# Conv feed-forwards and latent stage on normalized inputs: later splits, projections by token tile, gains in the weights

## The chip, the cores and the metric

The kernel runs on one core of a Trainium2 chip, as one program. The metric is the device time of one execution in microseconds (us); smaller is better. The engines are TensorE (PE in the profile; PEld are its weight loads), VectorE (DVE), ScalarE (ACT), GpSimd (POOL) and SyncE (SP), which starts the transfers of the weights. Each engine takes its own instructions in a fixed order and waits on semaphores for the others.

## What is computed

Two transformer blocks run one after the other on 256 tokens of width 1024, in fp32. The first has two layers of feed-forward, three-branch attention and feed-forward. The second has a convolutional mixer, a convolutional feed-forward, a latent attention and a second convolutional feed-forward. Cut to the parts that the change touches:

```
def conv_ffn(x_n, w_up, conv_w, w_down):            # w_up 1024 x 5632, w_down 2816 x 1024
    g, u = split(causal_dwconv(x_n @ w_up, conv_w)) # three taps along the tokens
    return (silu(g) * u) @ w_down

h = h + short_conv_mixer(rms_norm(h, a_mix_norm), ...)
h = h + conv_ffn(rms_norm(h, ffn_norm[0]), ...)
ckv = rms_norm(h, kv_in_norm) @ w_dkv               # 256 latent columns and 64 rope columns
k_nope, v = rms_norm(ckv[:256], kv_norm) @ w_ukv;   k_rope = rope(ckv[256:])
q = rms_norm(rms_norm(h, b_mix_norm) @ w_dq, q_norm) @ w_uq   # 8 heads, 128 + 64 rope
s = (q_nope . k_nope + q_rope . k_rope) * scale     # causal, one k_rope for all heads
h = h + (softmax(s) @ v) @ w_o
h = h + conv_ffn(rms_norm(h, ffn_norm[1]), ...)
return rms_norm(h, final_norm)
```

In the mixers of the first block one of the branches is stick-breaking attention: log-sigmoids of the scores are summed from the right along the keys, and the weights are the exponentials of those sums.

## The kernel before

**Products.** Every large product is made as three matmuls of numbers that are split into a high and a low part: `hi` x `acth`, `lo` x `acth` and `hi` x `actl`. The weights come in pieces of 512 KB. For each, SP starts the transfer to `raw`, ScalarE casts it to `hi` (line 270), VectorE subtracts (`lo`, line 271). There are five buffers for `raw` and eight each for `hi` and `lo`. Activations are split in the same way (lines 375 and 376, on ScalarE and on VectorE or POOL). The 256 tokens are two tiles of 128, t = 0 and t = 1. In the form of `mm_b` a product has the weights stationary and streams 256 token columns; in the form of `mm_a` the activations are stationary and 512 weight columns are streamed into the banks named `acc00`, `acc01` (t = 0) and `acc10`, `acc11` (t = 1). PSUM has four banks for products (tag mm), two for scores (z) and two for transposes (tr).

**Order.** TensorE's order is set by the Python code itself: a simulated clock `now` advances with each matmul group (`tick`), and side work stands in generators (`Task`) that give up control with a delay from the table `DELAY`. When the clock reaches a task's due time, its next part is emitted there. The other engines' orders come from the tile scheduler.

**Stick-breaking** (`stick_breaking`): scores of a key block and a query block for eight heads go into two z banks (line 592); ScalarE and VectorE make the log terms (lines 608 to 612, 585, `lnh` and `lnl` in 375 and 376); the last of them frees the bank. `sums` are matmuls with a triangle (line 624). In between stand the projections of the mixer, evicted as qs, ks, qf, kf (line 816). `sb_z`, `sb_ln` and so on are the delays between these steps.

**Conv feed-forward** (`conv_ffn`): the input is multiplied by the gain but not by the row factor r of the norm. Chunks c = 0 to 3 are made in `mm_a` form and transposed; chunks 4 to 21 in `mm_b` form, each into one bank `cf` (gate half and up half, 48 matmuls). VectorE multiplies it by r into `cgu` (line 972), where r lies along the columns in `rb`, which `across` makes with two diagonal matmuls (line 484). ScalarE multiplies by the last tap (line 877), VectorE adds the other two (line 879, 255 and 254 columns, for gate and up), ScalarE takes silu (line 945), POOL multiplies gate and up (line 946), and the product is split. Behind chunk 21 the down projection begins (`out_proj`): its four accumulators take the banks of chunks 18 to 21.

**Latent** (`latent`): `both` transposes h and makes two inputs, with the gains of the two norms. The first projections (`dkv`, 320 columns; `dq`, 512) run over both token tiles each, the row factor is applied behind them (`factor`), then come the norms, rope, transposes, `uk`, `uqr`, `uqn` and `uv`. `latent_half` and `latent_unit` make the scores: for each head a matmul of 128 rows (kn, line 1085) and one of 64 rows (kr, line 1086) into one z bank. `pre_gain` and `pre_norm` prepare the next stage's input at the end of `out_proj`; the delays `n_conv`, `n_ffnA`, `n_mla`, `n_ffn2` say how much later the transposes are asked for.

## Time and profile before

| quantity | value |
|---|---|
| median of three timed runs | 1906.56 us (1905.06 to 1908.55) |
| profiled execution | 1908.66 us |
| its span | 1906.9 us |
| mean granted TensorE clock | 0.991 of full speed |
| PE busy | 1868.0 us (98%) |
| DVE busy | 1260.4 us (66%) |
| ACT busy | 969.1 us (51%) |
| POOL busy | 256.7 us (13%) |

Busy time of TensorE is modelled from overlapping matmuls, so 98% does not say how much of it is useful: a matmul of 512 columns stands with about 0.4 us, while two of them begin 0.23 us apart. What TensorE loses is seen in the distance of starts, in its waits, and in stretches where the granted clock is below 1.

### The profile page before, as it was taken

The numbers are of one execution on the slowest core, as the hardware profiler recorded it, in microseconds if no ns is written. First come the engines' busy times: TensorE is split into PE (matmuls) and PEld (weight loads), VectorE is DVE, ScalarE is ACT, GpSimd is POOL, SyncE is SP. The second block draws the span as 40 slices with busy tenths as digits, with TensorE's granted clock in tenths as the row PEclk, the third lists the DMA queues.
The fourth block names the chain that finished last, engine by engine and source line by source line (L and its number), as shares of the span: only waits on it lengthen the run. The fifth ranks groups of instructions, "written<-read, shape, count | busy, mean of one in ns | idle before, by whom it ended". The sixth has DMA issues, their size and how long they took to land.

```text
span 1906.9 us, 30378 instructions
## 1 busy us (share of the span) xinstructions
PE 1868.0 (98%) x11990; PEld 1674.8 (88%) x11990; DVE 1260.4 (66%) x1682; ACT 969.1 (51%) x1483; POOL 256.7 (13%) x231
## 2 busy tenths in 40 slices
PE   8999999999999999999999999999999989999988
PEld 7998998878899889989887889988989977889976
DVE  6664756766766476637776776647668756658763
ACT  6444545554644364436555464435456544547552
POOL 1000102002100010001200210001414313003320
PEclk9999999999999999999999999999999999999989
DMA  8655664335555565546443555545454444425551
GB/s 288 220 195 181 227 209 162 143 133 200 206 186 184 177 213 185 188 166 248 163 143 133 210 192 192 184 169 202 177 192 174 178 178 152 152 92 189 178 178 65
DMA packets 95358, 343.30 MB, mean 180 GB/s; under 512 B 10720, under 2 KB 10992, under 8 KB 95216
## 3 DMA queue, kind: packets, MB, share of 16 engines
q1 hardware_dynamic: 95216, 341.37, 51.3%
q8 instruction: 94, 1.54, 0.3%
q14 instruction: 48, 0.39, 0.1%
HBM read 339.21 MB, written 2.11 MB: 179 GB/s over the span
## 4 chain that ended last, share of the span: by engine, by line
PE 84%; DVE 7%; ACT 3%; POOL 3%; issue 2%; DMA 0%; DVEq 0%; SPq 0%; ACTq 0%; POOLq 0%
PE acc L287 14%; PE acc L290 14%; PE acc L288 14%; PE gu L299 7%; PE gu L300 7%; PE gu L298 7%; DVE lo L271 3%; PE mm L298 3%; PE mm L299 3%; PE mm L300 3%; DVE cy L879 2%; ACT hi L270 2%; POOL cy L946 2%; PE tr L383 2%; PE cv L300 1%
## 5 line engine op out<-in xcount | busy, mean ns | idle before, releaser
L271 DVE TENSOR_TENSOR lo<-raw,hi 128x1024 fp32r<-128x1024 f32 (+3 forms) x616 | 759.3, 1241 | 342.4 <-ACT hi L270 340.8
L270 ACT CAST hi<-raw 128x1024 fp32r<-128x1024 f32 (+3 forms) x616 | 639.5, 1043 | 451.1 <-PE acc L290 218.5
L287 PE MATMUL acc<-hi,acth 128*128 128x512 f32 x1200 | 483.8, 403 | 12.6 <-DVE cgu L972 11.0
L288 PE MATMUL acc<-lo,acth 128*128 128x512 f32 x1200 | 476.3, 397 | 0.2 <-DVE lo L271 0.2
L290 PE MATMUL acc<-hi,actl 128*128 128x512 f32 x1200 | 388.2, 397 | 0.6 <-DVE actl L376 0.5
L300 PE MATMUL gu<-acth,lo 128*128 128x256 f32 x1152 | 323.8, 281 | 0.0
L299 PE MATMUL gu<-actl,hi 128*128 128x256 f32 x1152 | 323.6, 281 | 0.0
L298 PE MATMUL gu<-acth,hi 128*128 128x256 f32 x1152 | 323.3, 281 | 0.0
L287 PEld LDWEIGHTS acc<-hi,acth 128*128 128x128 f32 x1200 | 227.5, 190 | 67.8 <-DVE cgu L972 12.3
L290 PEld LDWEIGHTS acc<-hi,actl 128*128 128x128 f32 x1200 | 227.0, 189 | 55.6 <-DVE actl L376 2.3
L288 PEld LDWEIGHTS acc<-lo,acth 128*128 128x128 f32 x1200 | 227.3, 189 | 50.5 <-DVE lo L271 0.9
L298 PEld LDWEIGHTS gu<-acth,hi 128*128 128x128 f32 x1152 | 216.9, 188 | 0.2
L299 PEld LDWEIGHTS gu<-actl,hi 128*128 128x128 f32 x1152 | 216.8, 188 | 0.2
L300 PEld LDWEIGHTS gu<-acth,lo 128*128 128x128 f32 x1152 | 216.8, 188 | 0.0
L400 POOL TENSOR_TENSOR r<-v,mhalf 128x1 f32<-128x1 f32 x40 | 51.3, 1281 | 931.4 <-DVE v L397 923.1
L298 PE MATMUL cf<-acth,hi 128*128 128x256 f32 x576 | 162.1, 282 | 0.0
L300 PE MATMUL cf<-acth,lo 128*128 128x256 f32 x576 | 161.9, 281 | 0.0
L299 PE MATMUL cf<-actl,hi 128*128 128x256 f32 x576 | 161.8, 281 | 0.0
L298 PE MATMUL mm<-acth,hi 128*128 128x256 f32 x432 | 124.0, 287 | 0.0
L300 PE MATMUL mm<-acth,lo 128*128 128x256 f32 x432 | 122.6, 284 | 0.0
L299 PE MATMUL mm<-actl,hi 128*128 128x256 f32 x432 | 122.5, 284 | 0.0
L298 PEld LDWEIGHTS cf<-acth,hi 128*128 128x128 f32 x576 | 108.5, 188 | 0.1
(235 smaller groups left out, 2302.5 us busy)
## 6 DMA issues: line engine op xcount, KB each, us to landing
raw<-ffn_gu SPq DMA_DIRECT2D x175, 512.0 KB, 3.8
raw<-ffn_dn SPq DMA_DIRECT2D x88, 512.0 KB, 3.3
raw<-cf_up SPq DMA_DIRECT2D x88, 512.0 KB, 3.5
raw<-gate SPq DMA_DIRECT2D x48, 512.0 KB, 3.2
raw<-cf_dn SPq DMA_DIRECT2D x44, 512.0 KB, 3.4
raw<-a_in SPq DMA_DIRECT2D x18, 512.0 KB, 4.6
gain<-gains SPq DMA_DIRECT2D x17, 512.0 KB, 5.1
raw<-in_v SPq DMA_DIRECT2D x16, 516.0 KB, 3.3
```

The source lines that it names most:

```text
L270: self.last_hi = nc.scalar.copy(out=hi[:, cs], in_=raw[:, cs])
L271: nc.vector.tensor_tensor(out=lo[:, cs], in0=raw[:, cs], in1=hi[:, cs].bitcast(F32), op=ALU.subtract)
L287: nc.tensor.matmul(ps, x.h(k, ts), hi[:, cs], start=first, stop=False)
L288: nc.tensor.matmul(ps, x.h(k, ts), lo[:, cs], start=False, stop=False)
L290: nc.tensor.matmul(ps, x.l(k, ts), hi[:, cs], start=False, stop=last)
L298: nc.tensor.matmul(ps, hi[:, c], x.h(k), start=k == 0, stop=False)
L299: nc.tensor.matmul(ps, hi[:, c], x.l(k), start=False, stop=False)
L300: nc.tensor.matmul(ps, lo[:, c], x.h(k), start=False, stop=k == nk - 1)
L383: self.nc.tensor.transpose(ps[:, w * P:w * P + P], n[:, c * P:c * P + P], self.ident)
L400: nc.gpsimd.tensor_tensor(out=r, in0=v, in1=self.mhalf, op=ALU.pow)
L879: nc.vector.scalar_tensor_tensor(out=y[:, i:], in0=ps[:, :S - i], scalar=w[2 - i], in1=y[:, i:], op0=ALU.mult, op1=ALU.add)
L946: nc.gpsimd.tensor_tensor(out=y[:, 0], in0=y[:, 0], in1=y[:, 1], op=ALU.mult)
```

## The change

The change has five parts.

- **Delays.** In the table, `sb_z` goes from 9000 to 13000 and `sb_ln` from 9000 to 6000; `merge`, `n_conv`, `n_ffnA`, `n_mla`, `kv`, `q` and `lat_gap` change, `n_ffn2` is set apart for each layer (8300 and 6500), and `cf_gated` and `cf_split` are new. In the mixer's merge one of two additions moves from POOL to VectorE.
- **Conv feed-forward.** The input is normalized in full (`pre_norm`), so `r`, `across` and the product into `cgu` go. The convolution reads the PSUM bank itself. Its last-tap products stand first for gate and up, then both other taps of gate, then both of up. The product of gate and up and its split are tasks of their own. The down projection takes the first four chunks of t = 0 before t = 1 (`head=4`).
- **Latent input.** `plain` makes one normalized input; the gains of the two norms go into the weights (`take_gained`). `dkv` and `dq` run on t = 0, then on t = 1.
- **Latent rope.** The rope part of the keys is doubled before rope; `uqr` runs for each token tile by itself.
- **Latent scores.** They are made for two heads at a time, u = 0 and u = 1, in two z banks; the two 64-row matmuls, on the upper and the lower rows, stand next to each other. `latent_out` sets the order of the output projection.

```diff
-    DELAY = dict(..., merge=4600, ..., sb_z=9000, sb_ln=9000, ...
-                 cf_gap=4100, kv=6700, q=2600, rope=5600, lat_gap=2200, lat_p=9000, n_conv=4000, n_ffnA=1500,
-                 n_mla=3000, ..., n_ffn2=8300)
+    DELAY = dict(..., merge=3000, ..., sb_z=13000, sb_ln=6000, ...
+                 cf_gap=4100, cf_gated=2000, cf_split=9500, kv=5500, q=4000, rope=5600, lat_gap=6000, lat_p=9000, n_conv=9000,
+                 n_ffnA=5500, n_mla=7500, ..., n_ffn20=8300, n_ffn21=6500)
...
+    def take_gained(self, src, i, gains, w):
...
+        for j, g in enumerate(gains):
+            cs = slice(j * w, j * w + w)
+            nc.scalar.mul(out=hi[:, cs], in_=raw[:, cs], mul=g)
+            nc.vector.scalar_tensor_tensor(out=lo[:, cs], in0=raw[:, cs], scalar=g, in1=hi[:, cs].bitcast(F32),
+                                           op0=ALU.mult, op1=ALU.subtract)
...
-                        nc.gpsimd.tensor_tensor(out=gates[0][t][:, cs], in0=gates[0][t][:, cs], in1=y, op=ALU.add)
+                        (nc.gpsimd if i == 1 else nc.vector).tensor_tensor(out=gates[0][t][:, cs], in0=gates[0][t][:, cs], in1=y, op=ALU.add)
...
         def finish(c, gu):
             y = self.t2(name="cy", shape=(2, S))
-            for i in range(2):
-                self.conv3(y[:, i], gu[:, i], PP_FCONV + 132 * l + 3 * (c + KF * i))
+            for part in (self.conv3_last, self.conv3_rest):
+                for i in range(2):
+                    part(y[:, i], gu[:, i], PP_FCONV + 132 * l + 3 * (c + KF * i))
             nc.scalar.activation(out=y[:, 0], in_=y[:, 0], func=AF.Silu)
+            made[c] = [self.spawn(gated(c, y), self.DELAY["cf_gated"])]
+
+        def gated(c, y):
             nc.gpsimd.tensor_tensor(out=y[:, 0], in0=y[:, 0], in1=y[:, 1], op=ALU.mult)
+            yield self.DELAY["cf_split"]
             self.split([d[:, 0] for d in hT.blocks(c, 1)], y[:, 0], nc.gpsimd)
...
-            gu = self.t2(name="cgu", shape=(2, S))
-            nc.vector.tensor_tensor(out=gu, in0=bank, in1=rb, op=ALU.mult)
-            finish(c, gu)
-        return self.out_proj(dsrc, KF, hT, None, nxt)
+            finish(c, bank)
+        return self.out_proj(dsrc, KF, hT, None, nxt, before=made, head=4)
...
+        for t in range(NT):
+            self.join(ready[t])
+            for i, (src, per, w, g0, then, tasks) in enumerate(((s_dkv, 3, 320, PP_KV, kv, tkv), (s_dq, 2, 512, PP_Q, qlat, tq))):
+                chunks = kept[i] if t else [lambda i=i, c=c: keep(i, c) for c in self.whole(src, KD, per, gains=g0)]
+                tasks.append(self.spawn(then(t, rows(x, chunks, t, w))))
...
-            nc.tensor.matmul(z[:, i], qn[e][:, j, t * P:t * P + P], kn[e][:, j, :n], start=True, stop=False)
-            nc.tensor.matmul(z[:, i], qr[rows, j, t * P:t * P + P], kr[rows, :n], start=False, stop=True)
+                for u in range(2):
+                    nc.tensor.matmul(zs[u][:, i], qn[e][:, 2 * i + u, ts], kn[e][:, 2 * i + u, :n], start=True, stop=False)
+                for u in range(2):
+                    rows = slice(64 * u, 64 * u + 64)
+                    nc.tensor.matmul(zs[u][:, i], qr[rows, 2 * e + i, ts], kr[rows, :n], start=False, stop=True)
...
+        x2, g2 = Act(self, KD), self.gain("ffnA")
+        ready = self.conv_mixer(*state, lambda t: self.pre_norm(t, g2, x2, self.DELAY["n_conv"]))
...
+        def plain(t):
+            r = self.row_rstd(self.h[t])
+            ns = [self.nrm() for _ in range(2)]
+            for a in range(2):
+                nc.scalar.mul(out=ns[a], in_=self.h[t][:, a * 512:a * 512 + 512], mul=r)
             yield self.DELAY["n_ffnA"]
+            for a in range(2):
+                self.transpose_split(ns[a], x3.part(4 * a, 4, t))
```

**The order on TensorE, stick-breaking of the first layer.** The first z matmuls of the scores (0,1) stand on TensorE behind these products; `mm_3161` and `mm_3224` are the banks of two neighbouring blocks of the projections. Before:

```order
L298 MATMUL mm_3161<-acth_146,hi_3187 128x256
L299 MATMUL mm_3161<-actl_148,hi_3187 128x256
L300 MATMUL mm_3161<-acth_146,lo_3188 128x256
L592 MATMUL z_3198<-qs_2781,ks_2925 128x128
L592 MATMUL z_3199<-qs_2781,ks_2925 128x128
```

After:

```order
L313 MATMUL mm_3224<-acth_147,hi_3219 128x256
L314 MATMUL mm_3224<-actl_149,hi_3219 128x256
L315 MATMUL mm_3224<-acth_147,lo_3220 128x256
L609 MATMUL z_3243<-qs_2781,ks_2925 128x128
L609 MATMUL z_3244<-qs_2781,ks_2925 128x128
```

The scores moved from the middle of one block into the next one, 36 matmuls of 256 columns later.

**The order on VectorE at the same place.** `lnl_3083` is the operation that frees the second of the two z banks; lb and z with the number 3081 and 3061 are of the scores ahead, those with 3208 and 3198 (3253 and 3243) of the scores (0,1). Before:

```order
L611 SCALAR_TENSOR_TENSOR lb_3081<-z_3061,lb_3081 128x512
L612 TENSOR_TENSOR z_3061<-lb_3081,z_3061 128x512
L271 TENSOR_TENSOR lo_3495<-raw_3493,hi_3494 128x1024
L585 TENSOR_TENSOR z_3061<-z_3061,cst_88 128x512
L376 TENSOR_TENSOR lnl_3083<-z_3061,lnh_3082 128x512
L611 SCALAR_TENSOR_TENSOR lb_3208<-z_3198,lb_3208 128x512
L816 SCALAR_TENSOR_TENSOR qf_3092<-mm_3161,rb_2563 128x512
```

After:

```order
L628 SCALAR_TENSOR_TENSOR lb_3081<-z_3061,lb_3081 128x512
L629 TENSOR_TENSOR z_3061<-lb_3081,z_3061 128x512
L271 TENSOR_TENSOR lo_3495<-raw_3493,hi_3494 128x1024
L602 TENSOR_TENSOR z_3061<-z_3061,cst_88 128x512
L833 SCALAR_TENSOR_TENSOR qf_3092<-mm_3161,rb_2563 128x512
L271 TENSOR_TENSOR lo_3526<-raw_3524,hi_3525 128x1024
L393 TENSOR_TENSOR lnl_3083<-z_3061,lnh_3082 128x512
```

One eviction (qf) and one `lo` now stand ahead of `lnl_3083`.

**The order on VectorE, one round of the conv feed-forward's stream.** `cy` is a chunk's convolution, gate and up halves in turn. Before:

```order
L879 SCALAR_TENSOR_TENSOR cy_14705<-cgu_14703,pp_89,cy_14705 128x255 x2
L879 SCALAR_TENSOR_TENSOR cy_14705<-cgu_14703,pp_89,cy_14705 128x254 x2
L271 TENSOR_TENSOR lo_15015<-raw_15013,hi_15014 128x1024
L972 TENSOR_TENSOR cgu_14777<-cf_14716,rb_13948 128x512
L271 TENSOR_TENSOR lo_15045<-raw_15043,hi_15044 128x1024
```

After:

```order
L898 SCALAR_TENSOR_TENSOR cy_14814<-cf_14750,pp_89,cy_14814 128x255
L898 SCALAR_TENSOR_TENSOR cy_14814<-cf_14750,pp_89,cy_14814 128x254
L898 SCALAR_TENSOR_TENSOR cy_14814<-cf_14750,pp_89,cy_14814 128x255
L898 SCALAR_TENSOR_TENSOR cy_14814<-cf_14750,pp_89,cy_14814 128x254
L271 TENSOR_TENSOR lo_15113<-raw_15111,hi_15112 128x1024
L271 TENSOR_TENSOR lo_15146<-raw_15144,hi_15145 128x1024
```

The product into `cgu` is gone, the multiply-adds alternate in another way and read the bank, and the two `lo` of a round are neighbours. On ScalarE the order of a round is the same in both kernels: last taps, `hi`, silu, `acth`, `hi`.

## Rows read from the trace of the kernel before

**Rows 1.** Waits of TensorE: line, who ended them, total us, times, longest

```profile
PE acc L287 <- DVE cgu L972: 11.0, 3, 5.2
PE z L592 <- DVE lnl L376: 6.4, 2, 3.2
...
PE tr L383 <- DVE kr L1019: 1.8, 1, 1.8
...
PE tr L383 <- DVE cp L895: 1.0, 1, 1.0
PE tr L383 <- DVE h L459: 0.9, 1, 0.9
...
PE tr L383 <- ACT cb L896: 0.7, 1, 0.7
...
PE ca L287 <- ACT acth L375: 0.5, 1, 0.5
```

**Rows 2.** Stretches: busy us (instructions) of PE, PEld, DVE, ACT, POOL; PEclk; DMA

```profile
300.00:320.00 20.00, 16.80 (x125) 16.28 (x124) 12.54 (x16) 11.08 (x17) 0.00 (x0) 0.83 0.29 103
920.00:940.00 20.00, 16.80 (x133) 16.28 (x132) 13.26 (x17) 10.99 (x17) 0.00 (x0) 0.91 0.31 106
...
1320.00:1340.00 20.00, 18.30 (x136) 17.63 (x135) 13.86 (x21) 9.59 (x15) 5.82 (x5) 0.91 0.66 241
...
1595.00:1620.00 25.00, 21.43 (x107) 17.78 (x106) 21.39 (x38) 12.87 (x24) 13.27 (x20) 0.93 0.58 192
```

**Rows 3.** Timeline of PE, first layer: start, us, instruction, count, idle before

```profile
305.40 0.48 PE L592 MATMUL z<-qs,ks 64*128 64x128 f32 x2
```

**Rows 4.** Timeline of DVE, stick-breaking of the first layer

```profile
305.77 1.23 DVE L271 TENSOR_TENSOR lo<-raw,hi 128x1024 fp32r<-128x1024 f32 x1 [0.22 <-ACT hi L270]
...
308.25 0.69 DVE L376 TENSOR_TENSOR lnl<-z,lnh 128x512 fp32r<-128x512 f32 x1 [0.65 <-ACT lnh L375]
...
345.51 0.69 DVE L376 TENSOR_TENSOR lnl<-z,lnh 128x512 fp32r<-128x512 f32 x1 [0.65 <-ACT lnh L375]
346.46 1.29 DVE L626 TENSOR_TENSOR lb<-tr,lb 128x512 f32<-128x512 f32 x2 [0.25 <-PE tr L624]
```

**Rows 5.** Timeline of PE, conv mixer: the matmuls of one across

```profile
1324.21 0.61 PE L484 MATMUL tr<-diag,ones 128*128 128x128 f32 x4
```

**Rows 6.** Timeline of PE: scores of fox heads, then of latent heads

```profile
357.93 1.16 PE L592 MATMUL z<-kf,qf 64*128 64x128 f32 x16
...
1644.99 0.49 PE L1085 MATMUL z<-kn,qn 128*128 128x128 f32 x2
1645.41 0.48 PE L1086 MATMUL z<-kr,qr 64*128 64x128 f32 x2
```

**Rows 7.** Timeline of PE: last chunk of the first conv feed-forward, down projection

```profile
1526.84 0.28 PE L300 MATMUL cf<-acth,lo 128*128 128x256 f32 x1
...
1528.26 0.28 PE L300 MATMUL cf<-acth,lo 128*128 128x256 f32 x1
...
1535.53 0.80 PE L287 MATMUL acc<-hi,acth 128*128 128x512 f32 x1 [5.14 <-DVE cgu L972]
```

**Rows 8.** Timeline of DVE in the last rounds of that stream

```profile
1532.08 1.66 DVE L879 SCALAR_TENSOR_TENSOR cy<-cgu,pp,cy 128x255 f32<-128x255 f32 x4
1533.66 1.22 DVE L271 TENSOR_TENSOR lo<-raw,hi 128x1024 fp32r<-128x1024 f32 x1
1534.79 0.68 DVE L972 TENSOR_TENSOR cgu<-cf,rb 128x512 f32<-128x512 f32 x1
...
1538.02 1.66 DVE L879 SCALAR_TENSOR_TENSOR cy<-cgu,pp,cy 128x255 f32<-128x255 f32 x4
```

**Rows 9.** Timeline of POOL in the same rounds

```profile
1533.93 1.52 POOL L946 TENSOR_TENSOR cy<-cy 128x256 f32<-128x256 f32 x1 [3.15 <-ACT cy L945]
```

**Rows 10.** Timeline of DVE, conv mixer: two multiply-adds, the second on the first's result

```profile
1335.89 1.00 DVE L879 SCALAR_TENSOR_TENSOR cz<-cp,pp,cz 128x255 f32<-128x255 f32 x2 [1.17 <-ACT cz L877]
```

**Rows 11.** Timeline of POOL behind the first mixer: the power of a norm

```profile
486.97 6.01 POOL L400 TENSOR_TENSOR r<-v,mhalf 128x1 f32<-128x1 f32 x1 [5.18 <-DVE v L397]
```

More of the change, by code (lines that the diff above doesn't have):

```diff
@@ L354, in rows_a, with whole @@
             done(t)
-    def whole(self, src, nk, per=1, parts=1):
+    def whole(self, src, nk, per=1, parts=1, gains=None):
         kept = {}
@@ L361, in one @@
             if k % per == 0:
-                kept[0] = self.take(src, k // per, parts if k == 0 else 1)
+                g = gains and [self.pp[:, gains + j:gains + j + 1] for j in range(k, min(k + per, nk))]
+                kept[0] = self.take(src, k // per, parts if k == 0 else 1) if g is None else self.take_gained(src, k // per, g, src.shape[2] // per)
             w = src.shape[2] // per
@@ L1040, in latent @@
         self.join(*tq)
[L1041 to L1050 removed]
+        tr.append(self.spawn(qrope(1, rows(cq, uqr, 1, 512))))
         qn = [self.t4(name="qn") for _ in range(2)]
@@ L1056, in latent @@
         self.v_done = []
-        att = [self.spawn(self.latent_half(0, qn, kn, qr, kr, v, x))]
+        units, second = [[], []], []
+        scores = self.spawn(self.latent_scores(units, second, qn, kn, qr, kr, v, x))
+        self.cols_b(s_uqn, range(4, 8), cq, 4, 2, put(qn, nc.scalar.copy))
+        second.append(True)
         ps3, outs3 = self.banks(2)
@@ L1078, in latent_unit @@
[L1078 to L1089 removed]
+        return self.latent_out(s_o, x, units, nxt)
@@ new lines, in latent_out, with row, then @@
+    def latent_out(self, src, x, units, nxt):
+        ps, outs = self.banks(2)
+        chunks, held, tasks, done = self.whole(src, KD), [], [], [0, 0]
+        made = lambda e: len(units[e]) == 4 and not any(t.alive for t in units[e])
+        def row(t, os=None, k=None):
+            if k is None:
+                k = done[t]
+                done[t] += 1
+            if k == len(held):
+                held.append(chunks[k]())
+            self.mm_a(os or outs[t], x, k, t, *held[k], first=k == 0, last=k == KD - 1)
+        def then(t):
+            self.residual(t, ps[t], None)
+            yield from nxt(t)
+        self.until(lambda: made(0))
+        for k in range(4):
+            row(0)
+        while done[1] < 4 and not made(1):
+            row(1)
+        self.until(lambda: made(1))
+        for t in range(NT):
+            while done[t] < KD - self.FINE:
+                row(t)
+            for o in outs[t]:
+                for k in range(KD - self.FINE, KD):
+                    row(t, [o], k)
+            tasks.append(self.spawn(then(t)))
+        return tasks
@@ L1092, in latent_unit @@
             yield 400
-        h0 = 4 * e + j0
-        yield from self.weighted("lat", p, sums, nh, n, lambda a, i: v[a][:, h0 + i], P, x.part(h0, nh, t))
+        ts = slice(t * P, n)
+        yield from self.weighted("lat", p, sums, 2, n, lambda a, i: v[a][:, 4 * e + 2 * i + u], P, [y[e][:, u:4:2, ts] for y in (x.hi, x.lo)])
     def run(self, out):
```

155 lines of the change are left out of this document (73 added, 82 removed).

## The prediction

> **What bounds the kernel now.** The profiled execution took 1908.66 us with a span of 1906.9 us; the median of the three timed runs is 1906.56 us, 2.1 us less. I make the sum against 1908.66 and take 2.1 us off at the end. TensorE is the bound nearly everywhere: in the stream of a conv feed-forward two starts of 256-column matmuls lie 0.118 us apart, twelve of them from 1526.84 to 1528.26 [rows 7], and nothing on other engines shows as a wait. So only what shortens TensorE's own work, or the places where it stands, can pay. I read the waits of TensorE first [rows 1]. The reader should see that few places hold most of them: three waits of the down projection (acc) for a DVE operation of the conv feed-forwards, cgu, 11.0 us; two of the stick-breaking scores (z) for lnl, 6.4 us; then the conv mixer's head (cp, cb) and the latent stage's (kr). Second view, the same stretches with the granted clock [rows 2]: after each stop the mean clock of the stretch is below 1, so a wait costs more than its length. For 300 to 320 that is 3.2 us of waiting and up to 0.17 x 20 = 3.4 us of slower clock.
>
> **Stick-breaking, both layers.** The scores of block (0,1) move behind 36 more 256-column matmuls, 36 x 0.118 = 4.2 us. They need two z banks, and the second is freed by the lnl that begins at 308.25 and ends at 308.94 [rows 4]. Without the stop TensorE would come there 4.2 us later than the 305.4 of before [rows 3], at 309.6. If lnl stayed where it is, the whole wait would go. It does not stay: the order of the changed kernel puts one more eviction (qf) and one more lo ahead of it. That lo can run only when TensorE has given a weight buffer back. At TensorE's pace, one piece of weights per 24 matmuls or 2.8 us, it comes 2.8 us after the lo of 305.77 [rows 4], at 308.6, and lnl ends at about 308.6 + 1.2 + 0.7 = 310.5. So 0.9 us of the wait stays. Behind it the sums of (0,0) keep their place while the scores (0,0) come 6 matmuls, 0.7 us, later; there the last lnl ends at 346.20 and its reader's result is there at 346.46 [rows 4], so the margin is about nil and some 0.7 us of new waiting is likely. Per layer I count 2.5 us left. Before, waiting and clock cost 6.6 us in the first layer and 3.2 + 0.09 x 20 = 5.0 in the second: together a gain of 4.1 + 2.5 = 6.6, **take -7**, bounds 0 (the wait moves whole) and -10.
>
> **Conv mixer's head.** The layer-1 FFN's last transposes come earlier on TensorE's order, those of cp and cb 20 matmuls later (some 2.2 us of cover against waits of 1.0 and 0.7). With 0.5 for the transposed normal rows and 0.09 x 20 = 1.8 us of clock [rows 1, 2] that is 4.0; leaving 0.4, **-3.6**, bounds -4 and 0. Merge: one addition goes from POOL to DVE and the transposes come 6 matmuls earlier in each mixer; no row prices that, so I take for each the 0.5 that TensorE waited for acth at the conv mixer [rows 1]: **-1**, bounds -1.5 and 0. Two "across" steps go, each one group of four diag matmul records, 0.61 us [rows 5]: **-1**.
>
> **Latent stage.** The rows hold one normalized input in place of two gained ones, and the first projections run on one token tile and then the other, so the work of tile 0 covers the chain of tile 1. The stretch 1595 to 1620 lost 1.8 us to kr, 0.9 to h, and 0.07 x 25 = 1.8 to the clock [rows 1, 2]: 4.5. Each chain (squares, power, scaling, rope, transposes) is still there and fits its cover by 0 to 2 us, so I leave 0.8: **-3.7**, bounds -4.5 and +1. The scores: a kr matmul has 64 rows. Before, each stands between two full-height ones and takes 0.42 us from start to start, as the kn ones do [rows 6]. In the fox heads pairs on the two row halves run side by side: 16 records, eight pairs, in 1.16 us [rows 6]. The change makes such pairs of kr: 8 x 0.42 become 4 x 0.42 for tile 0, 1.7 us saved, and for tile 1, at twice the columns, between 1.7 and twice that. **Take -4.5**, bounds 0 (they accumulate on another matmul's result, which no pair of before does) and -6.
>
> **Later transposes at two boundaries.** The normal rows of the conv feed-forwards are now transposed at the end of the stage ahead (n_conv, n_mla), and TensorE takes the first acth right behind them, as at the conv mixer's head, where it waited 0.5: **+0.7 each, +1.4**, bounds 0 and +4.
>
> **The conv feed-forwards.** This is the large unknown. TensorE makes a chunk in 48 x 0.118 = 5.68 us. The other engines need 5.94 us: the multiply-adds of one chunk begin at 1532.08, those of the next at 1538.02 [rows 8]. So they fall behind by 0.26 us a chunk, and at the end the down projection, which needs the four banks, stands 5.14 us [rows 7] until cgu of the last chunk has read its bank at 1534.79 to 1535.47 [rows 8]. The round is a ring in order of the engines' own programs: acth, hi, lo, the four multiply-adds, silu, POOL's product, acth. cgu, 0.68 us, is not in it, so its removal shortens nothing there. Two things change. (a) The multiply-adds come in the order gate, gate, up, up: each second one needs the first one's result. A dependent pair takes 1.00 us [rows 10], four independent ones 1.66 [rows 8]; four in the new order make about 1.90, and POOL now follows the last of them instead of silu on the third. The product starts at 1532.08 + 1.90 + 0.06 = 1534.04 where it started at 1533.93; lo stands directly behind the multiply-adds as before (1533.66, 0.08 before their end), so it would run from 1533.90 to 1535.12, and the product ends 0.57 after lo, as it does now (1535.45 against 1534.88 [rows 8, 9]): 1535.69, 0.24 later. The ring grows to **6.18 us**. That splits are asked for later (cf_gated, cf_split) doesn't break it: in the built order of ScalarE, acth still stands directly behind silu. (b) A bank is now free after the last multiply-add and not after cgu: at 1539.68 instead of 1535.47 [rows 8], 4.2 us later, and the ring adds 0.24 x 13 = 3.1 over the 13 last chunks, in which the lag grows steadily. So the last bank comes at 1542.8. Against that stands the new order of the down projection: 18 more matmuls of 512 columns on the first two banks, 18 x 0.236 = 4.3 us, so TensorE, which came at 1535.53 - 5.14 = 1530.4, arrives at 1534.7 and stands 8.1 us instead of 5.14. **+3.0 in each feed-forward, +6**. If the multiply-adds kept 1.66, the release is at 1539.7 and the wait 5.0: no change. If POOL's product were not held up (0.74), the ring would fit into 5.68 and the wait would be gone.
>
> **Sum.** -7 - 3.6 - 1 - 1 - 3.7 - 4.5 + 1.4 + 6 = -13.4, so 1895.3 us on the profiled execution's scale and **1893 us** on that of the median.
>
> **Rivals.** *One: the lag in the conv feed-forwards goes away.* For it: lo A may come behind the product where hi is late, and multiply-adds that read PSUM may leave POOL alone. Against: lo has its operands before the multiply-adds end. It would give back the two long waits, 5.14 and 5.2, and by the clock after the stick-breaking waits some 4 us more, instead of +6: 1893 - 20 = 1873. *Two: the stick-breaking wait moves whole* to its sums or stays: 1900. *Three, slower: POOL's product is held up by two lo in a row.* In the new order lo A and lo B are neighbours on DVE, since cgu no longer parts them, and POOL waits long behind such rows: the power for a norm took 6.01 us at 486.97 [rows 11]. Then the ring is 6.18 + 1.23 = 7.41, another 1.23 x 13 = 16 us per feed-forward, 1893 + 32 = 1925; it decides from a ring of about 6.8 us on (26 x 0.66 = 17). Against it: lo B needs hi B, which on ScalarE stands behind acth, which needs the product. *Four: the power starves.* The new normalization puts it on the way at three boundaries, up to 5.5 us more each: 1893 + 16 = 1909, no change. Against it: behind the power's input on DVE stand the scalings that need its result, with one lo between at most, so there is no row of lo to wait for. The Trainium skill, page "SBUF — State Buffer", section "SBUF: two separate sides", says that the port pair shared by VectorE and GpSimd is an exclusive lock: whichever starts first has it for the whole instruction. By that the power would wait for one lo, 1.2 us, and 1909 would be 1897; the 6.01 us of [rows 11] is longer than any one lo, so the trace does not agree here, and I keep 5.5 as the bound.
>
> **How the numbers follow.** About 0.2%, 3.8 us, is what a measurement of this kernel can tell from no change. Chances: the forecast 0.58 (its own range 1885 to 1901), rival one 0.14, two 0.12, three 0.07, four 0.09. Faster: the first three, less a part of two, 0.83; within 0.2%: four and that part, 0.08; slower: three, and four with other costs at their upper bounds, 0.09. For 8 in 10 the range takes in rival one's partial form and two with the boundaries at their upper bounds, up to just below no change: 1875 to 1906.
>
> **What would show it.** Right: two stick-breaking waits under 1.5 us each; acth to acth 6.1 to 6.3 us in the conv feed-forwards and waits of acc for the last multiply-add of 7 to 10 us; kr matmuls starting in pairs; no waits for cp and cb. Wrong: acc waits under 3 us (rival one), TensorE standing inside the cf stream (three), rows of the power above 3 us followed by a wait of tr (four).

## The result and the profile after

The changed kernel takes 1896.57 us (median of four runs, 1895.62 to 1896.99), the kernel before 1906.89 us beside it. The ratio is 0.9945 with a 95% interval of 0.9928 to 0.9963: 10.3 us or 0.55% faster. The forecast was 1893 us, 13.6 us faster than before. The profiled execution of the changed kernel took 1896.99 us.

The head of the page of the changed kernel:

```profile
span 1895.2 us, 30338 instructions
...
PE 1858.4 (98%) x11982; PEld 1665.5 (88%) x11982; DVE 1235.9 (65%) x1657; ACT 966.7 (51%) x1496; POOL 228.5 (12%) x205
```

The waits of TensorE in the changed kernel, to be held against [rows 1] (line, who ended them, total us, times, longest):

```profile
PE acc L302 <- DVE cy L898: 11.8, 3, 5.5
...
PE z L1147 <- ACT p L576: 2.6, 3, 1.4
PE acc L305 <- DVE actl L393: 1.8, 4, 0.9
PE tr L641 <- DVE lnl L393: 1.7, 4, 0.6
PE acc L302 <- ACT acth L392: 1.6, 3, 0.7
PE tr L595 <- DVE actl L393: 0.9, 1, 0.9
PE z L609 <- DVE lnl L393: 0.9, 2, 0.4
...
PE tr L641 <- ACT lnh L392: 0.6, 2, 0.3
```

The waits for kr, cp, cb and h are gone, z for lnl is down from 6.4 to 0.9. The long wait of the down projections stays (11.8 against 11.0), now for the last multiply-add of a chunk. New are waits of the latent scores for the softmax (p). The stretches in question, as in [rows 2] (busy us of PE, PEld, DVE, ACT, POOL, then PEclk, the granted clock as a share of 2.4 GHz):

```profile
300.00:320.00 20.00, 19.57 (x164) 18.98 (x163) 15.66 (x21) 12.02 (x18) 0.00 (x0) 1.00 0.41 138
920.00:940.00 20.00, 19.56 (x165) 18.97 (x164) 15.18 (x20) 12.24 (x18) 0.00 (x0) 1.00 0.47 158
1300.00:1320.00 20.00, 20.00 (x138) 18.44 (x137) 16.24 (x23) 14.03 (x20) 1.38 (x2) 1.00 0.84 287
1520.00:1540.00 20.00, 14.42 (x54) 10.99 (x53) 11.98 (x15) 9.83 (x15) 4.26 (x5) 0.83 0.46 158
1640.00:1660.00 20.00, 15.84 (x79) 10.70 (x79) 13.14 (x35) 10.39 (x35) 0.00 (x0) 0.91 0.23 79
1680.00:1700.00 20.00, 18.46 (x81) 14.56 (x80) 12.77 (x18) 8.70 (x16) 2.02 (x2) 0.91 0.33 107
```

The clock is full where stick-breaking and the conv mixer's head slowed it before, and below 1 in two new places, 1640 to 1660 and 1680 to 1700. At the down projection (1520 to 1540) it is 0.83 in both kernels.

Where the time went, by stage. For each I took the start of the last addition into h (VectorE, the residual of t = 1) in both traces; the column on the right is what the stage gained (-) or lost (+):

| stage | before ends | after ends | gain of the stage | predicted |
|---|---|---|---|---|
| mixer, layer 0, from 207.84 / 208.54 | 500.01 | 496.50 | -4.2 | -4.6 |
| mixer, layer 1, from 861.51 / 857.90 | 1122.11 | 1114.49 | -4.0 | -3.4 |
| FFN of layer 1 and conv mixer | 1401.18 | 1391.12 | -2.4 | -3.6 |
| conv feed-forward 0 | 1600.36 | 1588.96 | -1.3 | +3.2 |
| latent | 1702.64 | 1688.38 | -2.9 | -8.2 |
| conv feed-forward 1 | 1900.08 | 1888.41 | +2.6 | +3.2 |

The predicted column puts the terms of the sum where they fall: half of each -1 (merge, across) and of +6 and +1.4 on each of the two places. For the start of the second mixer I took the addition of t = 0 (861.51 and 857.90). By the starts of the same matmuls on TensorE the two mixers gain 4.4 and 3.7 us, so the reading holds.

TensorE's starts also show where the time was won. The first cf matmul of conv feed-forward 0 (chunk 4) stands at 1424.54 us before and at 1414.06 after, 10.5 us earlier, and the whole span is 11.7 us shorter. Nearly all of the gain lies ahead of that matmul; in the conv feed-forwards and the latent stage, which the change rebuilt most, gains and losses nearly cancel.

**Stick-breaking.** VectorE, then TensorE, first layer of the changed kernel:

```profile
308.46 0.69 DVE L833 SCALAR_TENSOR_TENSOR qf<-mm,rb 128x512 f32<-128x512 f32 x1
309.42 1.23 DVE L271 TENSOR_TENSOR lo<-raw,hi 128x1024 fp32r<-128x1024 f32 x1 [0.27 <-ACT hi L270]
310.56 0.68 DVE L393 TENSOR_TENSOR lnl<-z,lnh 128x512 fp32r<-128x512 f32 x1
```

```profile
311.40 1.13 PE L609 MATMUL z<-qs,ks 64*128 64x128 f32 x14 [0.43 <-DVE lnl L393]
...
342.90 0.51 PE L641 MATMUL tr<-lnh,tri 128*128 128x512 f32 x1 [0.34 <-ACT lnh L392]
343.94 0.51 PE L641 MATMUL tr<-lnl,tri 128*128 128x512 f32 x1 [0.54 <-DVE lnl L393]
```

The eviction and the lo that now stand ahead of lnl are there, and the scores wait 0.43 us where they waited up to 3.2. The sums of (0,0) now wait, 0.34 and 0.54.

**The round of the conv feed-forwards.** VectorE, POOL and TensorE at the end of the first one's stream:

```profile
1521.81 1.90 DVE L898 SCALAR_TENSOR_TENSOR cy<-cf,pp,cy 128x255 f32<-128x255 f32 x4
1523.62 1.22 DVE L271 TENSOR_TENSOR lo<-raw,hi 128x1024 fp32r<-128x1024 f32 x1
...
1527.98 1.90 DVE L898 SCALAR_TENSOR_TENSOR cy<-cf,pp,cy 128x255 f32<-128x255 f32 x4
```

```profile
1523.85 1.57 POOL L978 TENSOR_TENSOR cy<-cy 128x256 f32<-128x256 f32 x1 [3.35 <-DVE cy L898]
...
1530.02 0.72 POOL L978 TENSOR_TENSOR cy<-cy 128x256 f32<-128x256 f32 x1 [3.35 <-DVE cy L898]
```

```profile
1524.17 0.39 PE L303 MATMUL acc<-lo,acth 128*128 128x512 f32 x1
1530.02 0.77 PE L302 MATMUL acc<-hi,acth 128*128 128x512 f32 x1 [5.47 <-DVE cy L898]
```

The four multiply-adds take 1.90 us, a round 6.17 us, as worked out. POOL's product takes 1.57 us with a lo beside it and 0.72 in the last round, which has no lo behind its multiply-adds. The acth that needs the product starts on ScalarE at 1525.45 and 1530.78, right behind these two ends.

**Latent scores and the boundary behind them.** TensorE:

```profile
1627.25 0.49 PE L1150 MATMUL z<-kr,qr 64*128 64x128 f32 x4
...
1647.45 0.70 PE L1147 MATMUL z<-kn,qn 128*128 128x256 f32 x2 [0.70 <-ACT p L576]
1649.59 0.70 PE L1147 MATMUL z<-kn,qn 128*128 128x256 f32 x2 [1.43 <-ACT p L576]
...
1688.77 0.50 PE L302 MATMUL acc<-hi,acth 128*128 128x512 f32 x1 [0.66 <-ACT acth L392]
...
1690.85 0.95 PE L305 MATMUL acc<-hi,actl 128*128 128x512 f32 x2 [0.88 <-DVE actl L393]
1691.61 0.63 PE L302 MATMUL acc<-hi,acth 128*128 128x512 f32 x1
```

Four records of kr stand in 0.49 us, where two stood in 0.48 before [rows 6]: the pairs run side by side. But 20 us later the scores wait for banks that the softmax still reads. ScalarE, the end of the softmax of t = 0 (128 columns) in the second half of the heads, for which the scores of t = 1 wait at 1649.59:

```profile
1649.06 0.38 ACT L576 ACTIVATE p<-z,m 128x128 f32<-128x128 f32 x1
```

At the boundary to the second conv feed-forward TensorE waits twice, the granted clock falls to its lower level (1.2 GHz), and a matmul stands with 0.63 us that stands with 0.40 at 2.4 GHz.

### The profile page after: what moved, and what is told of

Same layout as the page of the kernel before. It is cut to its first block, busy times and chain, and to the rows that moved or that the text cites. A ratio compares the mean times of both kernels' runs of the same rounds, so it can differ in the third digit from the quotient of the medians.

```text
span 1895.2 us, 30338 instructions
## 1 busy us (share of the span) xinstructions
PE 1858.4 (98%) x11982; PEld 1665.5 (88%) x11982; DVE 1235.9 (65%) x1657; ACT 966.7 (51%) x1496; POOL 228.5 (12%) x205
## 4 chain that ended last, share of the span: by engine, by line
PE 39%; DVE 5%; issue 2%; ACT 2%; POOL 2%; DMA 0%; DVEq 0%; POOLq 0%; ACTq 0%
PE acc L302 7%; PE acc L305 7%; PE acc L303 6%; DVE cy L898 2%; POOL cy L978 2%; PE gu L314 2%; PE gu L315 2%; PE gu L313 2%; DVE lo L271 2%; ACT hi L270 2%; PE cf L314 2%; PE cf L315 2%; PE cf L313 2%; PE tr L400 1%; PE cv L314 1%
## 5 line engine op out<-in xcount | busy, mean ns | idle before, releaser
L271 DVE TENSOR_TENSOR lo<-raw,hi 128x1024 fp32r<-128x1024 f32 (+3 forms) x609 | 748.0, 1236 | 360.9 <-ACT hi L270 359.6
L270 ACT CAST hi<-raw 128x1024 fp32r<-128x1024 f32 (+3 forms) x609 | 633.1, 1044 | 439.6 <-PE acc L305 212.4
L302 PE MATMUL acc<-hi,acth 128*128 128x512 f32 x1176 | 473.8, 403 | 13.5 <-DVE cy L898 11.8
L303 PE MATMUL acc<-lo,acth 128*128 128x512 f32 x1176 | 466.3, 396 | 0.2 <-DVE lo L271 0.2
L305 PE MATMUL acc<-hi,actl 128*128 128x512 f32 x1176 | 378.9, 397 | 1.8 <-DVE actl L393 1.8
L302 PEld LDWEIGHTS acc<-hi,acth 128*128 128x128 f32 x1176 | 222.8, 189 | 68.0 <-ACT cy L974 13.5
L305 PEld LDWEIGHTS acc<-hi,actl 128*128 128x128 f32 x1176 | 221.9, 189 | 55.8 <-DVE actl L393 4.1
L303 PEld LDWEIGHTS acc<-lo,acth 128*128 128x128 f32 x1176 | 222.9, 190 | 49.5 <-DVE lo L271 0.9
```

The lines of the kernel that those rows point to most:

```text
L270: self.last_hi = nc.scalar.copy(out=hi[:, cs], in_=raw[:, cs])
L271: nc.vector.tensor_tensor(out=lo[:, cs], in0=raw[:, cs], in1=hi[:, cs].bitcast(F32), op=ALU.subtract)
L302: nc.tensor.matmul(ps, x.h(k, ts), hi[:, cs], start=first, stop=False)
L303: nc.tensor.matmul(ps, x.h(k, ts), lo[:, cs], start=False, stop=False)
L305: nc.tensor.matmul(ps, x.l(k, ts), hi[:, cs], start=False, stop=last)
```

## The experiments

Times of a job are compared by their ratio to the kernel before, which ran on the same chip in the same job. 0.001 of the ratio is 1.9 us. The changed kernel itself stands at 0.9945. "Lag" is the end of a chunk's last multiply-add minus the end of TensorE's matmuls of that chunk. The former is read from the trace; the latter is counted back from the last cf matmul in steps of 5.68 us. The cf streams of the two conv feed-forwards are cf0 and cf1. What is read from one trace is read from one execution.

### e1_interleave: the order of the taps

```diff
-            for part in (self.conv3_last, self.conv3_rest):
-                for i in range(2):
-                    part(y[:, i], gu[:, i], ...)
+            for i in range(2):
+                self.conv3_last(y[:, i], gu[:, i], ...)
+            for n in (1, 2):
+                for i in range(2):
+                    nc.vector.scalar_tensor_tensor(out=y[:, i, n:], in0=gu[:, i, :S - n], ..., in1=y[:, i, n:], ...)
```

> The changed kernel, but the taps of the conv feed-forward are issued gate, up, gate, up again (first both one-step taps, then both two-step taps), still from the PSUM bank. Theory R (the ring of ScalarE, VectorE and POOL sets how far the engines lag; POOL's product waits for the last multiply-add and is then held by the lo behind it): the four multiply-adds take 1.66 us instead of 1.90, the round shrinks from 6.19 to about 5.95 us, the lag at the last chunk falls by 0.24 x 13 = 3.1 us or more, the two waits of acc for cy fall from 5.5 to about 2.4 us, and the kernel gains 6 to 9 us: 1888 to 1891. Theory S (the wait is set by something else, for instance by when the weights or the first chunks arrive): waits stay above 4.5 us, 1895 to 1898.

It took 1896.84 us, ratio 0.9943 (0.9925 to 0.9960): no change, and within what theory S names. Yet the round did what theory R says. VectorE:

```profile
1507.10 1.65 DVE L976 SCALAR_TENSOR_TENSOR cy<-cf,pp,cy 128x255 f32<-128x255 f32 x4
...
1513.04 1.65 DVE L976 SCALAR_TENSOR_TENSOR cy<-cf,pp,cy 128x255 f32<-128x255 f32 x4
```

The round is 5.94 us. But at chunk 8 the lag was already 10.6 and 7.5 us in the two feed-forwards, against 5.2 and 5.9 in the changed kernel, since the scheduler set the first chunks in another order; at chunk 21 it came to 14.0 and 10.9, against 11.9 and 12.6. The waits of the two down projections went the same way: 7.5 and 4.8 us, against 5.5 and 6.3 in the changed kernel. So two numbers make the wait, the growth per round and the lag at the start of the stream, and my expectation had only the first.

### e2_gate_dve: the product on VectorE

```diff
-            nc.gpsimd.tensor_tensor(out=y[:, 0], in0=y[:, 0], in1=y[:, 1], op=ALU.mult)
+            nc.vector.tensor_tensor(out=y[:, 0], in0=y[:, 0], in1=y[:, 1], op=ALU.mult)
```

> The changed kernel with the product of gate and up on VectorE instead of POOL. In the built order it stands between the two lo of a round, and acth of a chunk stands behind the next chunk's last taps on ScalarE, so the ring is broken. Theory R: a round needs about 4.7 us of VectorE, less than TensorE's 5.68, the lag no longer grows, and the two waits of acc for cy fall under 1 us; with the slow clock behind them the kernel gains 12 to 16 us: 1881 to 1885. Rival S: the waits stay above 4.5 us and the time at 1895 to 1898. Rival V (VectorE gets too full, lo comes late, TensorE stands in the stream): over 1897.

It took 1880.19 us, ratio 0.9857 (0.9841 to 0.9873), some 17 us faster than the changed kernel. The waits of acc for cy are gone from the list. A round on VectorE:

```profile
1503.57 1.90 DVE L898 SCALAR_TENSOR_TENSOR cy<-cf,pp,cy 128x255 f32<-128x255 f32 x4
1505.39 1.22 DVE L271 TENSOR_TENSOR lo<-raw,hi 128x1024 fp32r<-128x1024 f32 x1
1506.53 0.42 DVE L978 TENSOR_TENSOR cy<-cy 128x256 f32<-128x256 f32 x1
1508.12 1.23 DVE L271 TENSOR_TENSOR lo<-raw,hi 128x1024 fp32r<-128x1024 f32 x1 [1.17 <-ACT hi L270]
```

VectorE is idle 1.17 us in the round, waiting for a hi that itself waits for TensorE: now TensorE leads, and the lag stands at 4.2 us from chunk 8 to chunk 21. Theory R holds, with a gain a little over what it named, and rivals S and V fall.

### e3_head0: without the cover

```diff
-        return self.out_proj(dsrc, KF, hT, None, nxt, before=made, head=4)
+        return self.out_proj(dsrc, KF, hT, None, nxt, before=made)
```

> The changed kernel without head=4 in the two down projections: t = 1 is asked for right behind the first chunk of t = 0, as in the kernel before. If those 18 matmuls are cover for the wait (theory R), the wait of acc for cy grows from 5.5 to about 9.8 us in each feed-forward and the kernel takes about 8.5 us more: 1904 to 1906. If the order of the down projection doesn't matter, it stays at 1896 to 1898.

It took 1905.72 us, ratio 0.9993 (0.9984 to 1.0003), 9 us more than the changed kernel. The lag is the same to 0.1 us (11.9 at chunk 21), and the waits grow:

```profile
PE acc L302 <- DVE cy L898: 19.3, 4, 5.0
```

The 18 matmuls are cover: by the times they are worth 4.5 us at each place, by the waits 3.8 (19.3 against 11.8 in all). Without them the rest of the change would have gained nothing that could be measured.

### e5_split0: product and split asked for at once

```diff
-cf_gated=2000, cf_split=9500
+cf_gated=0, cf_split=0
```

> The changed kernel with cf_gated and cf_split at 0: product and split are asked for at once. The lag of the multiply-adds behind TensorE was 7.6 us at chunk 8 before the change and 5.2 after it. Theory R1 (that came from the removed cgu and across, not from the later splits): lag at chunk 8 stays near 5.2, round 6.2, time 1895 to 1898. Theory R2 (the later splits made it): lag at chunk 8 goes to about 7 us, waits of acc for cy to 7 us or more, time 1899 to 1903.

It took 1897.07 us, ratio 0.9946 (0.9930 to 0.9961). The lag at chunk 8 was 6.4 and 6.5 us, between the two theories, and 13.1 and 13.3 at the end. The waits for cy rose from 11.8 to 13.3 us in all; the time didn't show it.

### e11_before_late: the later splits alone, in the kernel before

```diff
-            nc.gpsimd.tensor_tensor(out=y[:, 0], in0=y[:, 0], in1=y[:, 1], op=ALU.mult)
-            self.split([d[:, 0] for d in hT.blocks(c, 1)], y[:, 0], nc.gpsimd)
+            later[c] = [self.spawn(gated(c, y), 2000)]
+        def gated(c, y):
+            nc.gpsimd.tensor_tensor(out=y[:, 0], in0=y[:, 0], in1=y[:, 1], op=ALU.mult)
+            yield 9500
+            self.split([d[:, 0] for d in hT.blocks(c, 1)], y[:, 0], nc.gpsimd)
```

> The kernel before with one edit: product and split of a chunk in the conv feed-forwards are asked for later, as tasks with the change's delays (2000 and 9500). At chunk 8 the multiply-adds end 7.6 us behind TensorE before, 5.2 in the changed kernel, 6.4 in it without these delays. Theory R2 (later splits account for about half of the 2.4): lag at chunk 8 near 6.4, waits of acc for cgu 4 us instead of 5.2, 2 to 3 us gained. Theory R1 (the removed cgu and across made it): lag stays at 7.6 and the time within 1.5 us of the kernel before.

It took 1907.60 us, ratio 1.0009 (0.9999 to 1.0018): nothing gained. The lag at chunk 8 was 8.0 and 8.6 us (before: 7.6 and 8.6). Later splits alone don't lower the lag at the start in the kernel before, while in the changed kernel their absence raised it by about 1 us.

### e10_before_dve: the product on VectorE in the kernel before

The same one line as in e2, in the kernel before.

> The kernel before with one edit: the product of gate and up in the conv feed-forwards on VectorE instead of POOL. In its built order acth stays ahead of the next hi on ScalarE, so the ring stays closed: multiply-adds 1.57, lo 1.14, product 0.42, acth 0.35, hi 1.05, lo 1.26, about 5.8 us instead of 5.94 with TensorE at 5.68. Theory R: growth of the lag falls from 0.29 to about 0.1 us a chunk, the two waits of acc for cgu fall from 5.2 by 2 to 2.5 us each, and the kernel gains 4 to 7 us. If the product's engine alone did it (not the open ring), waits vanish and it gains 14 us.

It took 1894.15 us, ratio 0.9945 (0.9930 to 0.9960): 10.5 us faster than before, as much as the whole change. Its round:

```profile
1510.53 1.66 DVE L879 SCALAR_TENSOR_TENSOR cy<-cgu,pp,cy 128x255 f32<-128x255 f32 x4
1512.10 1.22 DVE L271 TENSOR_TENSOR lo<-raw,hi 128x1024 fp32r<-128x1024 f32 x1
1513.24 0.42 DVE L946 TENSOR_TENSOR cy<-cy 128x256 f32<-128x256 f32 x1
...
1516.23 1.66 DVE L879 SCALAR_TENSOR_TENSOR cy<-cgu,pp,cy 128x255 f32<-128x255 f32 x4
```

The ring is still closed, 5.70 us, but as short as TensorE's 5.68: the lag stays at 7.1 us, and each wait for cgu falls from 5.2 to at most 1.7 us, 3.5 us less. In the traces the two conv feed-forwards gain 5.6 and 7.2 us by the additions into h, and TensorE's waits ahead of the down projections account for 3.6 and 4.2 of it. The rest goes with the clock, which falls there in the kernel before and stays full here (PEclk behind the five busy times). Before, then e10:

```profile
1520.00:1540.00 20.00, 14.86 (x92) 13.22 (x91) 15.76 (x27) 11.81 (x20) 6.95 (x7) 0.83 0.47 175
1825.00:1845.00 20.00, 14.14 (x68) 11.56 (x67) 13.69 (x22) 11.64 (x20) 8.23 (x8) 0.74 0.51 174
```

```profile
1520.00:1540.00 20.00, 18.48 (x114) 16.22 (x113) 16.00 (x25) 12.38 (x20) 2.86 (x4) 1.00 0.56 184
1825.00:1845.00 20.00, 19.05 (x82) 15.45 (x83) 11.30 (x14) 10.14 (x13) 1.48 (x2) 1.00 0.64 189
```

I had expected 4 to 7 us, by the waits alone.

### e4_sb_only: the two stick-breaking delays alone, in the kernel before

```diff
-sb_z=9000, sb_ln=9000
+sb_z=13000, sb_ln=6000
```

> The kernel before with two delays of the change alone: sb_z 13000, sb_ln 6000, so the scores (0,1) of stick-breaking stand 36 matmuls later on TensorE. Theory (the prediction's term, 7 us): waits of z for lnl fall from 6.4 to about 1, small new waits at the sums of (0,0), and the kernel gains 6 to 8 us against the kernel before: 1899 to 1901. Rival (the gain between 300 and 490 us and between 920 and 1110 us of the changed kernel comes from the merge's edits): at most 3 us gained, 1904 or more.

It took 1902.38 us, ratio 0.9982 (0.9973 to 0.9991): 1.7 to 5.1 us faster. The waits are those of the changed kernel:

```profile
PE tr L624 <- DVE lnl L376: 1.8, 4, 0.6
...
PE z L592 <- DVE lnl L376: 0.9, 2, 0.4
```

In the traces the start of the last h addition moved by -3.2 us in the first mixer (from +0.2 to -3.0) and -3.5 in the second (from -2.8 to -6.3), 0.9 of which the following stage gave back. Mechanism right, size under what I expected. By the starts of the same matmuls on TensorE the two mixers gain 3.1 and 2.5 us here, and 4.4 and 3.7 in the changed kernel. The 2.5 us between the two sums are what is left for the edits of the merge; those were not run alone.

### e6_lat9: latent scores further apart

```diff
-lat_gap=6000
+lat_gap=9000
```

> The changed kernel with lat_gap 9000 instead of 6000: the groups of latent scores stand further apart on TensorE. In the changed kernel the scores of the second half wait for the softmax of the first (z for p, 2.6 us, and a slow clock behind it, in all some 7 us between 1640 and 1660). Theory L (the groups come too close together for two z banks): waits of z for p fall under 0.7 us and the kernel gains 3 to 6 us: 1891 to 1894. Rival: the work that covers (projection of v, uqn) is used up before, so the waits only move to the output projection: within 1.5 us of 1896.6.

It took 1899.67 us, ratio 0.9970 (0.9960 to 0.9979), 5 us more than the changed kernel. The waits of z for p are gone, and these took their place:

```profile
PE tr L400 <- DVE p L586: 5.8, 2, 3.5
```

Theory L falls. The rival's reason holds, but not its time, within 1.5 us of the changed kernel. The work that covers the softmax is used up, so a later group of scores only means a later softmax. The scores that waited longest in the changed kernel are those of t = 1 in the second half, for the softmax of t = 0 in the same half. The expectation names the softmax of the first half, which was the shortest of the three waits (0.5 us).

### e8_nopair: the pairs taken apart

```diff
-                for u in range(2):
-                    rows = slice(64 * u, 64 * u + 64)
+                    rows = slice(64 * u, 64 * u + 64)
```

> The changed kernel with the score matmuls of the latent heads in the old alternation (kn, kr, kn, kr), so that the two 64-row matmuls no longer stand side by side. Theory P (the pairs run side by side and save TensorE 4.5 to 6 us, of which the new waits for the softmax ate a part): kr takes 0.42 (128 columns) and 0.63 us (256) each again, the waits of z for p shrink by part of that, and the kernel takes 2 to 5 us more: 1898.5 to 1901.5. Rival (pairs save nothing): within 1 us of 1896.6.

It took 1901.76 us, ratio 0.9982 (0.9971 to 0.9994), 7 us more than the changed kernel with an uncertainty of some 3 us; the two spans differ by 3.3 us (1898.5 against 1895.2). A kr matmul of one head takes its old time again:

```profile
1627.87 0.49 PE L1147 MATMUL z<-kn,qn 128*128 128x128 f32 x2
1628.29 0.48 PE L1149 MATMUL z<-kr,qr 64*128 64x128 f32 x2
```

By the starts, two heads at 256 columns take 1.6 us from their first kn matmul to the next (1634.39 to 1635.97 in the changed kernel) and 2.4 without pairs (1635.76 to 1638.16); at 128 columns it is about 1.1 against 1.7. For the eight heads that makes some 5.7 us. The waits of z for p fell from 2.6 to 1.2 us, and the clock is full here from 1640 to 1660. So the pairs save TensorE time, and part of it comes back as waiting for the softmax and as a slower clock behind it.

### e7_bound, e9_dve_bound: earlier transposes at the boundaries

```diff
-n_conv=9000, ... n_mla=7500
+n_conv=4000, ... n_mla=3000
```

> The changed kernel with n_conv 4000 and n_mla 3000, as before the change: the transposes of the next stage's input are asked for earlier. Theory B (their late place costs: 0.7 + 0.9 us of waits for acth and actl at 1688 and 1691 us, slow clock behind them, and 1.7 us of loss around 1388 to 1403): the kernel gains 3 to 5 us: 1892 to 1894. Rival (earlier they wait for the norm's result itself, since power and scaling are now on the way): 1896 or more, with waits of tr for nrm of over 2 us.

On the changed kernel it took 1894.25 us, ratio 0.9946 (0.9928 to 0.9964): no change. The waits for acth and actl are gone at both boundaries, and one for the norm's result came at the second:

```profile
PE tr L400 <- DVE nrm L435: 1.6, 1, 1.6
```

In the traces TensorE wins 1.9 us up to the first cf matmul and 1.3 at the second boundary, and loses 1.2 and 0.6 in the two down projections. The long wait there is 5.47 us, as in the changed kernel. So what was won did not come back as a longer wait, which the next expectation takes for given. What grew is the slow stretch behind the wait, some 0.8 us of loss at each place: the granted clock from 1530 to 1540 is 0.71 against 0.79, from 1831 to 1841 it is 0.74 against 0.82.

With the product on VectorE as well:

> The changed kernel with the product on VectorE and n_conv 4000, n_mla 3000. With POOL's product, earlier transposes at the two boundaries gained nothing on the clock of the whole (1894.3 against about 1895 by the same comparison): the 2 us won around 1390 came back as a longer wait for the last multiply-add. Theory G (the lag behind TensorE swallows what is won ahead of it; without the lag a win stays): now 2 to 4 us are gained on the same kernel with late transposes: a ratio to the kernel before of 0.984, 1876 to 1878. Rival (earlier transposes just wait for the norm's result): ratio 0.986 or more.

It took 1877.33 us, ratio 0.9855 (0.9840 to 0.9869), within the uncertainty of e2's 0.9857. The profiled spans are 1874.9 and 1880.2 us, of which 0.9 us lies at the start. By TensorE's starts 1.7 us are won up to the first cf matmul, 1.6 in the latent stage, where the clock is slow in e2 and full here, and 1.3 at the second boundary; in the down projections, where neither kernel waits, nothing is lost. That points to what theory G forecasts, a win that stays, though by the clock and not by the wait. By the ratios no gain can be told, so the runs don't settle it.

### e12_sums_later: the last stick-breaking wait, on the fastest version

```diff
-sb_last=13000
+sb_last=15500
```

> The fastest version so far (product on VectorE, n_conv 4000, n_mla 3000), and sb_last 15500 instead of 13000: the stick-breaking sums of (0,0) stand 12 512-column matmuls (2.8 us) later on TensorE. In the changed kernel they wait for lnl and lnh of scores that themselves moved back, 0.5 + 0.8 us in each layer by the distance of starts. Theory: these waits vanish (tr for lnl and lnh from 2.3 us to about 0.7) and the span falls by 2 to 3 us from 1874.9. Rival (the later sums move what comes behind them, the attention on kf and qf, into waits): the span stays at 1874 to 1877.

It took 1876.12 us, ratio 0.9842 (0.9825 to 0.9858), span 1871.8 us. The waits of the sums for lnl fell from 1.7 to 0.6 us:

```profile
PE tr L641 <- DVE lnl L393: 0.6, 2, 0.3
```

Of the 3.1 us between the spans TensorE's starts put 2.1 into the two mixers, 0.3 ahead of them and 0.8 into the latent stage, which this edit doesn't touch. So the mixers gain what the theory names, in one trace; by the ratios it can't be told from e9. This version has the lowest time of all: 30 us under the kernel before and some 20 under the changed one.

## Why the prediction was right, and where its steps were off

The sign, the size and the range held: 10.3 us gained against 13.4 in the sum. Two large terms were off by 5 us each in opposite directions and nearly cancelled. That the sum came as near as it did is luck; the direction is not, since the terms ahead of the conv feed-forwards held: 11.6 us forecast for those three stages, 10.6 measured. Of the signs that the prediction named, one did not come: waits of 7 to 10 us for the last multiply-add. They came to 5.5 and 6.3.

**Stick-breaking: right, a little large.** That lnl would move behind one more lo and leave a small wait was right: it ended at 311.24, forecast 310.5, and TensorE was 0.7 us later here from the start of the execution on. The new wait at the sums of (0,0) came as foreseen. The term was 7 us; e4 gives 1.7 to 5.1 by its runs and 5.3 by the traces up to the end of layer 1. The merge's term, -1, was too small by 1 to 1.5, if what e4 leaves of the mixers' gain is the merge's.

**Conv mixer's head: right mechanism, 1.2 us too large.** The waits for cp and cb are gone and the clock is full from 1300 to 1320; the stage gained 2.4 us where 3.6 were forecast. No run has this part alone.

**Conv feed-forwards: right ring, wrong start.** The round of 6.18 us was measured as 6.17 to 6.20. The growth of the lag that follows from it, 0.29 + 0.24 = 0.53 us a chunk, was measured as 0.52. The cause shows in the rows above: POOL's product takes 1.57 us beside a lo and 0.72 without. The Trainium skill, page "SBUF — State Buffer", section "SBUF: two separate sides", has the port pair shared by VectorE and GpSimd as an exclusive lock for the whole instruction. The rows agree with that: the product ends at 1525.42, 0.58 us after the lo's end. The cover of the down projection was right too (e3: 4.5 us a place, forecast 4.3). The step that failed is "So the last bank comes at 1542.8": it adds the ring's 3.1 us to the release of the kernel before, and with that takes over the lag at chunk 8 from there without a reason. In the changed kernel that lag is lower:

| kernel | lag at chunk 8 (cf0, cf1) | growth a chunk | lag at chunk 21 |
|---|---|---|---|
| before | 7.6, 8.6 | 0.29 | 11.3, 12.3 |
| changed | 5.2, 5.9 | 0.52 | 11.9, 12.6 |
| e1, taps interleaved | 10.6, 7.5 | 0.26 | 14.0, 10.9 |
| e2, product on VectorE | 4.3, 4.2 | 0.00 | 4.2, 4.2 |
| e5, splits at once | 6.4, 6.5 | 0.52 | 13.1, 13.3 |
| e10, before with the product on VectorE | 7.0, 7.2 | 0.02 | 7.1, 7.3 |
| e11, before with later splits | 8.0, 8.6 | 0.29 | 11.6, 12.3 |

So the wait became 5.47 us instead of 8.1, and both places together +0.8 (11.8 against 11.0) instead of +6. What lowers the lag at the start isn't settled. At chunk 4 it is 3 to 5 us in every kernel of the table; they part in chunks 5 to 8, between which the other engines also work on the transposed chunks 0 to 3. The table shows differences of up to 5 us between orders that the scheduler gave these chunks; the later splits account for about 1 us of it in the changed kernel and for nothing in the old one. The removal of cgu and across by themselves was not tried: without cgu the built order changed in other places too. The first conv feed-forward came out 4.5 us better than forecast, 2.7 of which are this wait; the rest no run accounts for.

**Latent: too large by 5 us.** The term -3.7 for the waits was right as to kr and h, which are gone, and the pairs do run side by side (e8); they save more than the 4.5 us of the term, some 5.7. What I missed is that the shorter scores and the new grouping by two heads bring each group of the second half up to the softmax of the group ahead, which still holds the two z banks: 2.6 us of waiting for p (2.1 of it t = 1 waiting for t = 0), 0.9 for actl, and a granted clock of 0.91 behind it (1640 to 1660), up to 1.8 us more. That rival wasn't on my list. e6 shows that a longer gap doesn't mend it; other orders were not tried.

**Boundaries: mis-sized.** For the one ahead of the second conv feed-forward I took 0.7, the wait for acth of the conv mixer. It waits 0.66 for acth, 0.88 for actl, and the clock of 0.91 from 1680 to 1700 costs up to another 1.8: about 3 us. From the last addition into h to the first cf matmul it is 26.4 us, before it was 22.9; so part of what the latent stage gained in the table is lost again right behind it. What I had not seen is that acth stands on ScalarE behind squares and hi of the other tile, and actl on VectorE behind lo. In conv feed-forward 0 the waits were 0.7 and 0.2, as forecast.

**The rivals.** Rival three (two lo in a row) didn't come, for the reason given: lo B waits for hi B behind acth. Rival four (the power starves) didn't either. The powers of the new norms on POOL in the changed kernel:

```profile
1683.59 0.56 POOL L417 TENSOR_TENSOR r<-v,mhalf 128x1 f32<-128x1 f32 x1 [58.74 <-DVE v L414]
1691.00 1.46 POOL L417 TENSOR_TENSOR r<-v,mhalf 128x1 f32<-128x1 f32 x1 [6.85 <-DVE v L414]
```

One is free and one waits for a single lo. At the other two boundaries the longest took 1.47 us. Rival two (the stick-breaking wait moves whole) did not come: 6.4 us became 0.9, and 2.3 at the sums. Rival one did not come by the change, but e2 shows what it would have been worth: some 17 us, where I had put 20.

## What to carry to other kernels

Where two or more in-order engines hand a tile around, write down the ring with each engine's own order, sum it, and compare it with the period of the engine that should lead; one 1.6 us product on the wrong engine decided here some 17 us. A wait at the end of such a stream is start lag plus growth times rounds, and the start lag must be read or forecast for itself. Before work is made cheaper, ask which later wait hides it: the paired scores saved some 5.7 us of TensorE's time, and a part came back as waiting for the softmax that the scores caught up with.

## What the hardware showed that I had not expected

- In the latent scores of the kernel before, a 64-row matmul between two 128-row ones takes 0.42 us from start to start, and so does its neighbour, at 128 columns and two records each [rows 6]; in a run of pairs of one shape a pair of records begins every 0.11 us (16 records in 1.16 us, [rows 6]), and the four records of across, all of 128 rows, take 0.61 us [rows 5]. So beside a change of shape a record takes twice the time: 0.21 us from start to start. The pairs have fewer such changes, which the prediction didn't count. The Trainium skill, page "TensorEngine Tiling (Array Packing)", section "Gotcha 1: PSUM Pressure", says that different row tiles write to different PSUM banks. The pairs here do so (u = 0 and u = 1 have a z bank each), and they run side by side (four records in 0.49 us) while accumulating on another matmul's result, which no pair of the kernel before did.
- The slow clock behind a wait can cost more than half of what the wait costs: in the traces the one-line edit of e10 takes 7.8 us of waiting off the two down projections and gains 12.8 us in the two stages, with the clock there at 1.00 instead of 0.83 and 0.74. By the runs it gained 10.5 us.
